# A two-layer encoder on one core: norms ahead of the first product's operands, x loaded by halves, three weight parts on VectorE, and one sum in a tile of its own

## The chip, the core and the metric

One core of one Trainium2 chip runs the whole program. Time is device time of one execution in microseconds (us), taken as the median of several runs. PE is the matmul engine (PEld its weight loads), DVE the vector engine, ACT the scalar engine, POOL GpSimd, SP the engine that issues the DMAs. Each engine works through its own list of instructions in order; an instruction that waits holds up all behind it on that engine.

## What is computed

Two layers on 512 tokens of 1024 channels in float32. Each layer is a half-step feed-forward block, a mixer of four attention kinds, and a second feed-forward block, each followed by a norm:

```python
def _swiglu(h, w_gu, w_down):
    gate, up = jnp.split(h @ w_gu, 2, axis=-1)
    return (jax.nn.silu(gate) * up) @ w_down

for l in range(DEPTH):
    x = _layer_norm(alpha * x + 0.5 * _swiglu(x, ffn_w_gu[l, 0], ffn_w_down[l, 0]), ln_g[l, 0], ln_b[l, 0])
    mix = _token_mixers(x, w_in[l], ..., w_out[l], l)
    x = _layer_norm(alpha * x + mix, ln_g[l, 1], ln_b[l, 1])
    x = _layer_norm(alpha * x + 0.5 * _swiglu(x, ffn_w_gu[l, 1], ffn_w_down[l, 1]), ln_g[l, 2], ln_b[l, 2])
```

`w_gu` is 1024 x 5632, `w_down` 2816 x 1024, `w_in` some 2500 columns wide, `w_out` 1024 x 1024.

## The kernel before

**Numbers.** A float32 product is made of three products of rounded parts: every operand is split into a high part (a cast on ACT: `al`, `wh`, `xTh`) and a low part (operand minus high part, on DVE: `al`, `wl`, `xTl`), and PE adds high·high, high·low and low·high.

**Stages.** Six stages follow one another: ffn(0,0) to about 358 us, mixer 0 to 612, ffn(0,1) to 958, ffn(1,0) to 1320, mixer 1 to 1575, ffn(1,1) to the end. x lies in four tiles of 128 tokens (x_86 to x_89 in the program's names, for t = 0 to 3).

**Gate and up product.** It is done by a seven-product scheme on 2 x 2 blocks. A `Pair(j)` stands for 256 columns of gate and 256 of up; its weights come in four tiles b11, b21 (gate) and b12, b22 (up), 512 KB each. `step1` and `step2` multiply b11 and b21 (banks ga, gb); `step5` first adds b12 to b11 in place (L458), `step6` adds b22 to b11 in place (L467), `step7` adds b22 to b12 (L475), `step3` takes b22, `step4` adds b11 to b21 (L490). Each step splits its operand (`parts4`: ACT cast L403, DVE low part L404, 128x1024 each) and issues 24 matmuls per half, 128x256 wide, spaced 0.12 us apart at full clock. The operands from x, `al[1]` to `al[7]`, are made by `to_al`: tiles t = 0, 1 give `al[1]`, `al[2]` (L181, L182), which steps 1 and 2 use; tiles t = 2, 3 give sums (L216 to L225) and `al[3]` to `al[7]` (L178, L179, L181, L182), which steps 5, 6, 7, 3 and 4 use. p0 and p1 are the pairs 0 and 1. At the start of an ffn the order is p0 steps 1, 2, p1 steps 1, 2, then the rest of p0 and the rest of p1.

**The ring.** `raw_tile` hands out weight buffers in turn; of every seven calls the 1st, 3rd and 5th come from pool `raw` (3 buffers), the others from tag `pt` of pool `blk` (4 buffers). p0 and p1 take eight tiles in the order b11, b21, b12, b22 of p0, then b11, b21, b12, b22 of p1, so seven are free of each other and the eighth reuses the first.

**Into an ffn.** `norm_to_al` (L339) is called for each tile when the stage before has finished it: sum and statistics on DVE (L348, L349, L331, L333), the power on GpSimd (L334, `rs`), one more factor on DVE (L351), the norm itself as two ACT instructions of 128x512 (L353), four PE transposes into `xtp`, and `to_al`. This is so at the entries of ffn(0,1) (called T1 here, about 605 to 660), ffn(1,0) (T2, 950 to 1012) and ffn(1,1) (T3, 1568 to 1625).

**Into a mixer.** The norm has four DVE products per tile (L320 twice, L327 twice), then `to_xT` (transposes, ACT L147, DVE L148). Meanwhile the mixer's first weight units are split; the low parts of units 5, 6 and 7 (`ON_POOL`) run on GpSimd (L239, 128x864, 128x576, 128x1024), the others on DVE.

**Order.** The order on each engine is set by a scheduler that takes the code's order, priorities (`tc.high_priority`) and data into account. At the opening SP loads x_86 and x_87 whole, then p0's four tiles, x_88, x_89, p1's b11 and b21.

## Time and profile before

| | |
|---|---|
| median of 3 runs | 1945.51 us (1944.58 to 1945.53) |
| the profiled execution | 1943.79 us, of which span 1942.0 us |
| PE busy | 1876.5 us, 97% of the span |
| DVE busy | 1697.9 us, 87% |
| ACT busy | 1061.1 us, 55% |
| POOL busy | 262.1 us, 13% |

The span is the profiler's; the 1.8 us between it and the execution's time lie around it. An engine's busy time says how full its list is; whether it is late is seen from the idle time before its instructions, which stands in square brackets in the timeline, with what ended it. PEclk is the share of full TensorE clock that was granted in a stretch: 1.00 is 2.4 GHz, 0.50 is 1.2 GHz.

### The profile page before, as it was taken

How to read it: one execution, taken by the hardware profiler on the slowest of the kernel's cores; microseconds unless marked ns; L12 is line 12 of the kernel's file. 1: busy time of each engine (PE TensorE's matmuls, PEld its weight loads, DVE VectorE, ACT ScalarE, POOL GpSimd, SP SyncE). 2: the span in 40 equal slices, each digit the busy share in tenths (PEclk: the TensorE clock that was granted, in tenths of full speed). 3: DMA queues.
4: the chain of work that ended last, by engine and by line, in shares of the span. 5: the costliest groups of instructions: out<-in, count | busy, mean ns of one | idle time of the engine just before them, and what ended most of it. 6: DMA issues, size and time to landing. Idle time of an engine off the chain costs nothing.

```text
span 1942.0 us, 32394 instructions
## 1 busy us (share of the span) xinstructions
PE 1876.5 (97%) x12252; PEld 1704.2 (88%) x12252; DVE 1697.9 (87%) x2733; ACT 1061.1 (55%) x1851; POOL 262.1 (13%) x387
## 2 busy tenths in 40 slices
PE   7999999999999899999989999999999999999998
PEld 6999998788878899999789999987887879999996
DVE  7999995858998999999499999957689989999985
ACT  5555554247776645555364555532587865455551
POOL 0000000345741000000000000004367300000001
PEclk9999999999999999999999999999999999999999
DMA  6333324243343334233232323241433334144221
GB/s 236 95 123 99 103 66 126 80 115 91 104 104 120 126 93 131 93 93 131 98 115 90 110 94 115 68 143 45 135 90 86 101 125 153 60 130 131 71 83 65
DMA packets 164413, 205.65 MB, mean 106 GB/s; under 512 B 15328, under 2 KB 123872, under 8 KB 164256
## 3 DMA queue, kind: packets, MB, share of 16 engines
q1 hardware_dynamic: 164256, 203.57, 34.0%
q8 instruction: 97, 1.59, 0.3%
q14 instruction: 60, 0.49, 0.1%
HBM read 178.49 MB, written 2.10 MB: 93 GB/s over the span
## 4 chain that ended last, share of the span: by engine, by line
PE 83%; DVE 9%; ACT 3%; POOL 2%; DMA 1%; issue 1%; SPq 0%; DVEq 0%; ACTq 0%; POOLq 0%
PE ga L266 26%; PE gc L266 13%; PE acc L266 9%; PE da L266 7%; PE gb L266 6%; PE nat L266 6%; PE dc L266 3%; PE sc L266 2%; PE pjt L266 2%; PE pv L266 2%; PE ptb L110 2%; PE db L266 2%; PE op L266 2%; DVE p L751 1%; PE xtp L110 1%
## 5 line engine op out<-in xcount | busy, mean ns | idle before, releaser
L403 ACT CAST wh<-b 128x1024 fp32r<-128x1024 f32 x300 | 313.1, 1053 | 287.3 <-DVE b L467 66.5
L266 PE MATMUL ga<-al,wh 128*128 128x256 f32 x2752 | 390.6, 285 | 4.4 <-ACT wh L403 4.4
L266 PEld LDWEIGHTS ga<-al,wh 128*128 128x128 f32 x2752 | 358.4, 192 | 16.1 <-ACT u L471 6.7
L404 DVE TENSOR_TENSOR wl<-b,wh 128x1024 fp32r<-128x1024 f32 x300 | 362.1, 1218 | 4.7 <-ACT wh L403 4.2
L266 PE MATMUL gc<-al,wh 128*128 128x256 f32 x1408 | 206.2, 289 | 20.5 <-ACT al L178 17.5
L266 PE MATMUL ga<-al,wl 128*128 128x256 f32 x1376 | 222.0, 284 | 1.0 <-DVE wl L404 1.0
L334 POOL TENSOR_TENSOR rs<-rs,mhalf 128x1 f32<-128x1 f32 x24 | 19.7, 819 | 1463.9 <-DVE rs L333 1459.7
L266 PEld LDWEIGHTS gc<-al,wh 128*128 128x128 f32 x1408 | 189.3, 197 | 24.3 <-ACT al L178 18.3
L266 PEld LDWEIGHTS ga<-al,wl 128*128 128x128 f32 x1376 | 190.3, 192 | 1.5 <-DVE wl L404 1.5
L540 ACT CAST wh<-d 128x512 fp32r<-128x512 f32 x168 | 98.0, 619 | 85.4 <-PE ga L266 40.8
L266 PE MATMUL acc<-wl,hh 128*128 128x512 f32 x320 | 125.3, 392 | 0.2 <-DVE wl L239 0.2
L266 PE MATMUL acc<-wh,hh 128*128 128x512 f32 x320 | 125.0, 391 | 0.0
L266 PE MATMUL acc<-wh,hl 128*128 128x512 f32 x320 | 124.9, 390 | 0.0
L239 DVE TENSOR_TENSOR wl<-wr,wh 128x1024 fp32r<-128x1024 f32 (+1 forms) x44 | 53.4, 1214 | 77.5 <-ACT wh L238 77.3
L266 PE MATMUL gc<-al,wl 128*128 128x256 f32 x704 | 118.7, 288 | 0.0
L238 ACT CAST wh<-wr 128x1024 fp32r<-128x1024 f32 (+2 forms) x50 | 50.8, 1025 | 109.4 <-PE acc L266 75.6
L541 DVE TENSOR_TENSOR wl<-d,wh 128x512 fp32r<-128x512 f32 x168 | 109.8, 683 | 0.3 <-ACT wh L540 0.2
L266 PE MATMUL da<-wh,dh 128*128 128x512 f32 x384 | 103.9, 392 | 0.0
L266 PEld LDWEIGHTS gc<-al,wl 128*128 128x128 f32 x704 | 101.3, 198 | 0.0
L793 ACT CAST pth<-ptb 128x512 fp32r<-128x512 f32 (+2 forms) x128 | 69.8, 545 | 41.7 <-PE ptb L110 40.5
L266 PE MATMUL gb<-al,wh 128*128 128x256 f32 x640 | 90.8, 283 | 0.5 <-ACT wh L403 0.5
L796 DVE TENSOR_TENSOR ptl<-ptb,pth 128x512 fp32r<-128x512 f32 (+2 forms) x128 | 80.6, 630 | 7.1 <-ACT pth L793 6.6
(320 smaller groups left out, 4148.9 us busy)
## 6 DMA issues: line engine op xcount, KB each, us to landing
b<-in_ffn_w_gu_dram SPq DMA_DIRECT2D x176, 512.0 KB, 4.6
d<-in_ffn_w_down_dram SPq DMA_DIRECT2D x96, 256.0 KB, 3.7
wr<-in_ffn_w_down_dram SPq DMA_DIRECT2D x40, 512.0 KB, 3.2
wr<-in_w_in_dram SPq DMA_DIRECT2D x30, 512.0 KB, 3.7
k<-ph SPq DMA_DIRECT2D x64, 128.0 KB, 2.3
wr<-in_w_out_dram SPq DMA_DIRECT2D x16, 512.0 KB, 3.3
qs<-ph SPq DMA_DIRECT2D x32, 128.0 KB, 2.4
ln_g<-in_ln_g_dram SPq DMA_DIRECT2D x14, 256.0 KB, 3.7
```

The source lines that it names most:

```text
L110: te.transpose(o, a, ident)
L238: se.copy(h[:, w], r[:, w])
L239: (lo or ve).tensor_tensor(l[:, q], r[:, q], h[:, q].bitcast(F32), op=ALU.subtract)
L266: te.matmul(o, a, b, start=start, stop=stop, **kw)
L334: ge.tensor_tensor(rs[:, 1:2], rs[:, 0:1], mhalf[:, 0:1], op=ALU.pow)
L403: se.copy(h, r[:, q])
L404: ve.tensor_tensor(lo, r[:, q], h.bitcast(F32), op=ALU.subtract)
L540: se.copy(wh[:, sl], self.r[rn][q])
L541: ve.tensor_tensor(wl[:, sl], self.r[rn][q], wh[:, sl].bitcast(F32), op=ALU.subtract)
L751: ve.tensor_tensor_reduce(p, sb, nd, -h.slope, h.sink[0] if h.sink else 3.0e38, ALU.add, ALU.min, m)
L793: se.copy(b.ph, b.tb[:, b.k0:b.k1])
L796: ve.tensor_tensor(b.pl, b.tb[:, b.k0:b.k1], b.ph.bitcast(F32), op=ALU.subtract)
```

## The change

1. In `norm_to_al` the sum, statistics and the two ACT instructions of the norm are scheduled with a priority raised by `NORMS = 120`.
2. At the opening, x of tiles 0 and 1 is loaded by halves of the channels (256 KB each): first halves, p0's b11, second halves, p0's b21; then p1's b11 and b21, x_88 and x_89, and p0's b12 and b22. `to_al` takes the groups it is to do, and `enter_half(g)` does one of them for both tiles ahead of step 1 and step 2.
3. `ON_POOL` is empty: the low parts of the mixers' units 5, 6 and 7 are made on DVE.
4. For pairs 0 and 1, `step6` writes its sum into a tile `t2` of its own, taken from the ring, instead of into b11; `step4` reads it there.

```diff
+    NORMS = 120
-    def turned_x(t):
-        bs = []
-        for g in range(2):
+    def turned_x(t, gs=range(2)):
+        for g in gs:
             b = bank4("pt", "xtp")
...
-    def to_al(t, gt=None):
+    def to_al(t, gt=None, gs=range(2)):
...
-            for g, b in turned_x(t):
+            for g, b in turned_x(t, gs):
...
-        stt = sm.tile([P, 2, 6], F32, tag="bn", name="bn", bufs=2)
...
+        with tc.high_priority(NORMS):
+            stt = sm.tile([P, 2, 6], F32, tag="bn", name="bn", bufs=2)
+            xs = [x[t][:, n * FD:(n + 1) * FD] for n in range(2)]
+            for n in range(2):
+                ve.scalar_tensor_tensor(xs[n], accs[n], c * INV_A, xs[n], op0=ALU.mult, op1=ALU.add)
+                ve.bn_stats(stt[:, n], xs[n])
+            rs, mv = norm_factors(stt)
+            ve.tensor_scalar(rs[:, 0:1], mv[:, 0:1], rs[:, 1:2], -1.0, op0=ALU.mult, op1=ALU.mult)
+            for n in range(2):
+                se.activation(xs[n], xs[n], AF.Identity, bias=rs[:, 0:1], scale=rs[:, 1:2])
         to_al(t, gained[0])
...
             def step6(self):
                 r = self.r
-                ve.tensor_tensor(r[11], r[11], r[22], op=ALU.add)
-                w = parts4(r[11])
+                r[6] = raw_tile("t2") if self.j < 2 else r[11]
+                ve.tensor_tensor(r[6], r[11], r[22], op=ALU.add)
+                w = parts4(r[6])
...
-                ve.tensor_tensor(r[21], r[21], r[11], op=ALU.add)
+                ve.tensor_tensor(r[21], r[21], r[6], op=ALU.add)
...
         if opening:
+            half, rest, consts = opening
+            opening.clear()
+            for g, n in ((0, 11), (1, 21)):
+                for t in range(2):
+                    load_half(t, g)
+                p0.load((n,))
+            p1.load((11, 21))
+            for t in range(2, NT):
+                load(x[t], d["x"][0, t * P:(t + 1) * P])
+            p0.load((12, 22))
+            half(0)
+            p0.step1(early[0])
+            half(1)
+            p0.step2(early[1])
+            rest()
+            p1.step1()
+            p1.step2()
+            consts()
...
-        ON_POOL = (5, 6, 7)
+        ON_POOL = ()
...
+    def load_half(t, g):
+        sl = slice(g * FD, (g + 1) * FD)
+        load(x[t][:, sl], d["x"][0, t * P:(t + 1) * P, sl])
+
+    def enter_half(g):
+        for t in range(2):
+            to_al(t, None, (g,))
```

In the changed file most lines of these functions are one further down (L353 becomes L354, L404 becomes L405, L467 becomes L468), while L454 and L458 keep their numbers.

**Mixer 0's entry, DVE**, around the norm of the last tile (x_89). Before:

```order
L316 BN_STATS bn<-x_89 128x6 [waits DVE_49]
L239 TENSOR_TENSOR wl<-wr,wh 128x864 [waits DMAHW7_49,DMAHW0_49]
L331 BN_AGGR mv<-bn 128x2 [waits DVE_49]
L333 TENSOR_SCALAR rs<-mv 128x1 [waits DVE_49]
L320 SCALAR_TENSOR_TENSOR x_89<-x_89,mv,ln_g 128x512 x2
L327 SCALAR_TENSOR_TENSOR x_89<-x_89,rs,ln_b 128x512 [waits DVE_49,Pool_49]
L327 SCALAR_TENSOR_TENSOR x_89<-x_89,rs,ln_b 128x512 [waits DVE_49]
```

Now:

```order
L316 BN_STATS bn<-x_89 128x6 [waits DVE_49]
L239 TENSOR_TENSOR wl<-wr,wh 128x864 [waits DMAHW2_49,DMAHW1_49]
L331 BN_AGGR mv<-bn 128x2 [waits DVE_49]
L239 TENSOR_TENSOR wl<-wr,wh 128x864 [waits DMAHW4_49,DMAHW3_49]
L333 TENSOR_SCALAR rs<-mv 128x1 [waits DVE_49]
L320 SCALAR_TENSOR_TENSOR x_89<-x_89,mv,ln_g 128x512 x2
L327 SCALAR_TENSOR_TENSOR x_89<-x_89,rs,ln_b 128x512 [waits DVE_49,Pool_49]
L327 SCALAR_TENSOR_TENSOR x_89<-x_89,rs,ln_b 128x512 [waits DVE_49]
L239 TENSOR_TENSOR wl<-wr,wh 128x576 [waits DMAHW6_49,DMAHW5_49]
L239 TENSOR_TENSOR wl<-wr,wh 128x1024 [waits DMAHW7_49,Activation_49]
```

Three low parts have come to DVE, one ahead of the four products of x_89's norm and two behind them; on GpSimd the three L239 rows are gone and the powers L334 follow one another. Mixer 1's entry reads the same.

**T2, DVE**, the norm factors of x_89 (L331, L333, then L351 before and L352 now) and the operands around them. Before:

```order
L331 BN_AGGR mv<-bn 128x2 [waits DVE_49]
L404 TENSOR_TENSOR wl<-b_10992,wh 128x1024 [waits Activation_49]
L179 TENSOR_TENSOR al_10594<-t_10814,al_10594 128x4x128 [waits Activation_49]
L220 TENSOR_TENSOR ac<-ac,t_10814 128x512 [waits DVE_49]
L333 TENSOR_SCALAR rs<-mv 128x1 [waits DVE_49]
L454 TENSOR_TENSOR s_10954<-gb,s_10954 128x512 [waits PE_49,Activation_49]
L225 TENSOR_TENSOR ac<-ac 128x512 [waits DVE_49]
L179 TENSOR_TENSOR al_10595<-ac,al_10595 128x4x128 [waits Activation_49]
L179 TENSOR_TENSOR al_10596<-t_10809,al_10596 128x4x128 [waits Activation_49]
L182 SCALAR_TENSOR_TENSOR al_10593<-a_10804,al_10593 128x4x128 [waits Activation_49]
L179 TENSOR_TENSOR al_10606<-ac,al_10605 128x2x128 [waits Activation_49]
L351 TENSOR_SCALAR rs<-mv,rs 128x1 [waits Pool_49]
```

Now:

```order
L349 SCALAR_TENSOR_TENSOR x_89<-acc_10370,x_89 128x512 [waits PE_49]
L350 BN_STATS bn<-x_89 128x6 [waits DVE_49]
L331 BN_AGGR mv<-bn 128x2 [waits DVE_49]
L333 TENSOR_SCALAR rs<-mv 128x1 [waits DVE_49]
L216 TENSOR_TENSOR t_10820<-t_10815,a_10810 128x512 [waits Activation_49]
L352 TENSOR_SCALAR rs<-mv,rs 128x1 [waits Pool_49]
L218 TENSOR_TENSOR t_10815<-t_10815,ac 128x512 [waits DVE_49]
L405 TENSOR_TENSOR wl<-b_10998,wh 128x1024 [waits Activation_49]
```

Between the aggregate and the last factor stood ten instructions, now two; the sum for p1's step 5 (L458) and the group of `al` parts stand behind.

**T1, DVE**, around the norm factors of x_88 (L333, L351; now L333, L352). Before:

```order
L333 TENSOR_SCALAR rs<-mv 128x1 [waits DVE_49]
L349 BN_STATS bn<-x_89 128x6 [waits DVE_49]
L182 SCALAR_TENSOR_TENSOR al_6952<-ac,al_6951 128x2x128 [waits DMAHW0_49,Activation_49]
L351 TENSOR_SCALAR rs<-mv,rs 128x1 [waits Pool_49]
L475 TENSOR_TENSOR b_7223<-b_7223,b_7225 128x1024 [waits DMAHW4_49]
L182 SCALAR_TENSOR_TENSOR al_6954<-ac,al_6953 128x2x128 [waits DMAHW6_49,DMAHW7_49,DMAHW0_49,Activation_49]
L348 SCALAR_TENSOR_TENSOR x_89<-op,x_89 128x512 [waits PE_49]
```

Now:

```order
L333 TENSOR_SCALAR rs<-mv 128x1 [waits DVE_49]
L468 TENSOR_TENSOR t_7397<-b_7223,b_7229 128x1024 [waits DMAHW6_49]
L352 TENSOR_SCALAR rs<-mv,rs 128x1 [waits Pool_49]
L350 BN_STATS bn<-x_89 128x6
L182 SCALAR_TENSOR_TENSOR al_6954<-ac,al_6953 128x2x128 [waits DMAHW1_49,DMAHW0_49,Activation_49]
L476 TENSOR_TENSOR b_7227<-b_7227,b_7229 128x1024
L349 SCALAR_TENSOR_TENSOR x_89<-op,x_89 128x512 [waits PE_49]
L182 SCALAR_TENSOR_TENSOR al_6956<-ac,al_6955 128x2x128 [waits DMAHW2_49,Activation_49]
L350 BN_STATS bn<-x_89 128x6 [waits DVE_49]
L182 SCALAR_TENSOR_TENSOR al_6958<-ac,al_6957 128x2x128 [waits DMAHW1_49,DMAHW2_49,DMAHW0_49,Activation_49]
L331 BN_AGGR mv<-bn 128x2 [waits DVE_49]
L491 TENSOR_TENSOR b_7225<-b_7225,t_7397 128x1024
```

The sums for p0's steps 6 and 4 (L468, L491) stand beside that of step 7 (L476) among the low parts of `al[1]` and `al[2]` of tile 1; before, L467 and L490 came 26 and 28 rows behind L475.

**T1, SP**: the weight loads of p1 (b_7298 and b_7296 are its b21 and b11, b_7519 its b12; now b_7302, b_7300 and b_7524, and b_7526 is its b22). Before, the three stood together:

```order
L94 DMA b_7298<-in_ffn_w_gu_dram 128x4x256 [waits DMAHW6_49,DVE_49,PE_49]
L94 DMA b_7296<-in_ffn_w_gu_dram 128x4x256 [waits DMAHW7_49,DMAHW1_49,DVE_49]
L94 DMA b_7519<-in_ffn_w_gu_dram 128x4x256 [waits DMAHW0_49,PE_49]
L94 DMA ln_b<-in_ln_b_dram 128x512
L94 DMA d<-in_ffn_w_down_dram 128x512 [waits DMAHW2_49]
```

Now, at that place and 13 rows further on:

```order
L96 DMA b_7302<-in_ffn_w_gu_dram 128x4x256 [waits DMAHW0_49,DVE_49,PE_49]
L96 DMA b_7300<-in_ffn_w_gu_dram 128x4x256 [waits DMAHW3_49,DMAHW1_49,DVE_49]
L96 DMA ln_b<-in_ln_b_dram 128x512 [waits DMAHW2_49]
L96 DMA d<-in_ffn_w_down_dram 128x512
L96 DMA d<-in_ffn_w_down_dram 128x512 [waits DMAHW4_49]
```

```order
L96 DMA ln_g<-in_ln_g_dram 128x512 [waits DMAHW5_49,DVE_49]
L96 DMA d<-in_ffn_w_down_dram 128x512 [waits DMAHW6_49,DVE_49,Activation_49]
L96 DMA b_7524<-in_ffn_w_gu_dram 128x4x256 [waits DMAHW7_49,DVE_49]
L96 DMA d<-in_ffn_w_down_dram 128x512 [waits DMAHW0_49,DVE_49]
L96 DMA b_7526<-in_ffn_w_gu_dram 128x4x256 [waits DMAHW1_49,DVE_49,PE_49]
```

The tile `t2` takes the ring's seventh buffer, which was that of p1's b12; b12 and b22 of p1 now reuse buffers of p0's b11 and b21 and are loaded after these are done with.

## Rows read from the trace of the kernel before

**Rows 1.** Page: busy time, share of the span and instructions of each engine.

```profile
PE 1876.5 (97%) x12252; PEld 1704.2 (88%) x12252; DVE 1697.9 (87%) x2733; ACT 1061.1 (55%) x1851; POOL 262.1 (13%) x387
```

**Rows 2.** Windows: stretch, length, busy time and count per engine, clock, DMA, GB/s.

```profile
0.00:20.00 20.00, 12.81 (x79) 11.88 (x80) 9.12 (x17) 11.56 (x22) 0.19 (x4) 1.00 0.94 340
...
366.00:369.00 3.00, 2.75 (x9) 2.40 (x10) 2.90 (x6) 0.59 (x1) 0.00 (x0) 0.50 0.29 84
...
643.00:649.00 6.00, 5.49 (x26) 5.35 (x26) 6.00 (x10) 4.56 (x8) 0.00 (x0) 0.50 0.60 182
...
700.00:800.00 100.00, 99.30 (x717) 93.67 (x716) 99.09 (x128) 50.73 (x71) 0.00 (x0) 1.00 0.32 100
```

**Rows 3.** DVE timeline at mixer 0's entry: start, duration, instruction, [idle before].

```profile
355.74 1.41 DVE L327 SCALAR_TENSOR_TENSOR x<-x,rs,ln_b 128x512 f32<-128x512 f32 x2
...
361.77 4.33 DVE L327 SCALAR_TENSOR_TENSOR x<-x,rs,ln_b 128x512 f32<-128x512 f32 x2
...
369.20 1.04 DVE L239 TENSOR_TENSOR wl<-wr,wh 128x864 fp32r<-128x864 f32 x1
...
371.78 1.41 DVE L327 SCALAR_TENSOR_TENSOR x<-x,rs,ln_b 128x512 f32<-128x512 f32 x2
375.24 0.69 DVE L148 TENSOR_TENSOR xTl<-xtp,xTh 128x512 fp32r<-128x512 f32 x1 [2.05 <-ACT xTh L147]
```

**Rows 4.** POOL timeline at mixer 0's entry.

```profile
361.64 3.91 POOL L239 TENSOR_TENSOR wl<-wr,wh 128x864 fp32r<-128x864 f32 x2
```

**Rows 5.** PE timeline at mixer 0's entry, its three groups of transposes that matter.

```profile
364.43 0.63 PE L110 MATMUL xtp<-ident,x 128*128 128x128 f32 x4 [1.45 <-DVE x L327]
366.25 1.09 PE L110 MATMUL xtp<-ident,x 128*128 128x128 f32 x4 [1.19 <-DVE x L327]
...
373.98 0.60 PE L110 MATMUL xtp<-ident,x 128*128 128x128 f32 x4
```

**Rows 6.** PE timeline of the opening, three instructions with idle time before them.

```profile
4.84 3.73 PE L110 MATMUL xtp<-ident,x 128*128 128x128 f32 x16 [4.84 <-DMA x<-in_x_dram]
10.92 2.78 PE L266 MATMUL ga<-al,we 128*128 128x256 f32 x10 [2.35 <-ACT we L403]
...
30.14 1.10 PE L266 MATMUL gc<-al,wh 128*128 128x256 f32 x7 [0.82 <-DVE al L179]
```

**Rows 7.** Page: DMA issues of the ffn's weights, KB each, median us to landing.

```profile
b<-in_ffn_w_gu_dram SPq DMA_DIRECT2D x176, 512.0 KB, 4.6
d<-in_ffn_w_down_dram SPq DMA_DIRECT2D x96, 256.0 KB, 3.7
```

**Rows 8.** DVE timeline of the opening: the low parts after p0's step 5 sum.

```profile
37.36 4.62 DVE L404 TENSOR_TENSOR wl<-b,wh 128x1024 fp32r<-128x1024 f32 x4
```

**Rows 9.** DVE timeline at T2.

```profile
949.61 1.23 DVE L458 TENSOR_TENSOR b<-b,b 128x1024 f32<-128x1024 f32 x1 [1.87 <-DMA b<-in_ffn_w_gu_dram]
...
976.96 0.69 DVE L348 SCALAR_TENSOR_TENSOR x<-acc,x 128x512 f32<-128x512 f32 x1
...
982.91 0.15 DVE L333 TENSOR_SCALAR rs<-mv 128x1 f32<-128x1 f32 x1
...
986.31 0.20 DVE L351 TENSOR_SCALAR rs<-mv,rs 128x1 f32<-128x1 f32 x1
```

**Rows 10.** PE timelines of T1 and T2, four instructions with idle time before them.

```profile
622.28 2.65 PE L266 MATMUL ga<-al,we 128*128 128x256 f32 x20 [0.45 <-DVE al L182]
...
642.55 0.58 PE L266 MATMUL gc<-al,wh 128*128 128x256 f32 x1 [5.25 <-ACT al L178]
...
993.81 0.58 PE L266 MATMUL gc<-al,wh 128*128 128x256 f32 x1 [4.43 <-ACT al L178]
995.51 1.86 PE L266 MATMUL gc<-al,wh 128*128 128x256 f32 x7 [1.11 <-DVE al L179]
```

**Rows 11.** DVE timeline at T1: one sum of 128x1024.

```profile
619.02 1.22 DVE L475 TENSOR_TENSOR b<-b,b 128x1024 f32<-128x1024 f32 x1
```

**Rows 12.** Line L334, the power on GpSimd: count, shortest/median/longest in ns, first and last start.

```profile
L334 POOL TENSOR_TENSOR rs<-rs,mhalf x24: 550/897/1473, 347.4 to 1936.4; 128x1 f32<-128x1 f32 x24
```

More of the change, by code (lines that the diff above doesn't have):

```diff
@@ L140, in turned_x @@
                 tr(b[:, k], x[t][:, (4 * g + k) * P:(4 * g + k + 1) * P])
-            bs.append(b)
             yield g, b
@@ L344, in norm_to_al @@
             gained[:] = [gt]
-        stt = sm.tile([P, 2, 6], F32, tag="bn", name="bn", bufs=2)
-        xs = [x[t][:, n * FD:(n + 1) * FD] for n in range(2)]
-        for n in range(2):
-            ve.scalar_tensor_tensor(xs[n], accs[n], c * INV_A, xs[n], op0=ALU.mult, op1=ALU.add)
-            ve.bn_stats(stt[:, n], xs[n])
-        rs, mv = norm_factors(stt)
-        ve.tensor_scalar(rs[:, 0:1], mv[:, 0:1], rs[:, 1:2], -1.0, op0=ALU.mult, op1=ALU.mult)
-        for n in range(2):
-            se.activation(xs[n], xs[n], AF.Identity, bias=rs[:, 0:1], scale=rs[:, 1:2])
+        with tc.high_priority(NORMS):
[8 more added lines that the diff above has]
+                se.activation(xs[n], xs[n], AF.Identity, bias=rs[:, 0:1], scale=rs[:, 1:2])
         to_al(t, gained[0])
@@ L427, in __init__, with load @@
                 self.j, self.w, self.r = j, {}, {}
-            def load(self, gate=True, up=True):
+            def load(self, ns=(11, 21, 12, 22)):
                 j = self.j
-                for n, k, u in ((11, 0, 0), (21, 1, 0), (12, 0, 1), (22, 1, 1)):
-                    if not (up if u else gate):
-                        continue
+                for n in ns:
+                    k, u = n // 10 - 1, n % 10 - 1
                     self.r[n] = raw_tile(f"b{n}")
@@ L589, in ffn @@
         if opening:
-            opening.pop(0)()
-        p0.load()
-        p0.step1(early[0])
-        p0.step2(early[1])
-        if opening:
-            opening.pop(0)()
-        p1.load(up=False)
-        p1.step1()
-        p1.step2()
-        if opening:
-            opening.pop(0)()
+            half, rest, consts = opening
[16 more added lines that the diff above has]
+            consts()
+        else:
+            p0.load()
+            p0.step1(early[0])
+            p0.step2(early[1])
+            p1.load((11, 21))
+            p1.step1()
+            p1.step2()
         for step in p0.rest():
             step()
-        p1.load(gate=False)
+        p1.load((12, 22))
         for step in p1.rest():
@@ L1624, in mixer, with enter_rest @@
         flush()
-    def enter(ts):
-        for t in ts:
-            load(x[t], d["x"][0, t * P:(t + 1) * P])
-        for t in ts:
+    def load_half(t, g):
[4 more added lines that the diff above has]
+            to_al(t, None, (g,))
+    def enter_rest():
+        for t in range(2, NT):
             to_al(t)
@@ L1636, in tile_encoder @@
     new_al()
-    opening = [lambda: enter((0, 1)), lambda: enter((2, 3)), constants]
+    opening = [enter_half, enter_rest, constants]
     for l in range(DEPTH):
```

## The prediction

> **What bounds the kernel now.** I read first the busy times, then the windows, then the idle times on each engine at the places that the change touches. PE is busy 1876.5 of 1942.0 us [rows 1], so at most 65.5 us of waiting can be won, and all of it at the seams of the stages: inside a feed-forward stage PE has 99.30 of 100 us at clock 1.00, with DVE beside it at 99.09 of 100 [rows 2]. So DVE is as full as PE there; what DVE loses in those stages is not made up. The places that matter are the opening, the two entries of the mixers, and T1, T2 and T3. The second thing to see is the clock: after idle time of 1.45 and 1.19 us [rows 5] the stretch 366 to 369 was granted 0.50, that is 1.2 instead of 2.4 GHz, and after 5.25 us [rows 10] the stretch 643 to 649 was too [rows 2]. So idle time is paid for twice. All sums are made against the profiled execution, 1943.79 us; the median of the runs shown is 1.7 us above it.
>
> **Three low parts to VectorE.** At mixer 0's entry the last two products of x_88's norm take 4.33 us; the same pair takes 1.41 before and after it [rows 3]. The difference, 2.92 us, lies under two L239 on GpSimd, 361.64 to 365.55 [rows 4]. PE waits for just these products, 1.45 + 1.19 = 2.64 us [rows 5]. Then it works at half clock: of the 2.75 us that it is busy in 366 to 369 [rows 2] about half, 1.4, is lost. That is 4.0 us; mixer 1 repeats these rows, so it is 8.0 for both, 8.1 with the last few tenths of the low clock. The edit takes GpSimd's products away, so the products of the norm should take 1.41 again. What comes onto DVE is one part of 128x864, 1.04 us [rows 3], one of 128x576 (0.7 by its size) and one of 128x1024 (1.22, as any of that size [rows 11]). Only the first stands ahead of x_89's norm. That norm ended at 373.19 [rows 3]; it now ends 2.92 sooner and about 0.95 later, at 371.2. PE transposed x_89 from 373.98, without waiting [rows 5]; 4.0 us less and four matmuls more ahead of it in the new order (0.2 each) bring it there at about 370.8 for the first half and 371.3 for the second, when they are ready. So the next wait is 0 to 0.1; if PE is there first, up to 0.9 per mixer. The other two parts fall into the 2.05 us in which DVE sat idle [rows 3]; without that cover they would cost 1.9 each time. **Mixers: -8.1, bounds -5 to -8.5.**
>
> **T2: norms ahead.** x_89's second sum starts at 976.96, but its statistics end only at 982.91, and the factor that ACT waits for comes at 986.31 [rows 9], because ten instructions stand between. Now two do: aggregate, L333, one 0.68 us sum, factor. That gives the factor at 976.96 plus 0.69 for the sum, as much for its statistics, 0.2 for the small ones and 0.9 for the power [rows 12], near 979.4, and the norm and the transposes of x_89 some 6.7 us sooner. The products of steps 1 and 2 end where they did (993.81 less 4.43, 989.4), since they hang on earlier tiles; PE then waited 4.43 + 1.11 us for the first sum of tiles 2 and 3 [rows 10]. Those operands are cast and subtracted in a list of some ten DVE and ACT instructions each, so they come not 6.7 but 3.3 us sooner (992.2 against 995.5). With the clock as low as before that is the gain, less 0.4 for a low part behind the later load (below): 2.9; with the clock kept, the other 23 matmuls of step 5 would save 0.1 us each, the spacing of 0.13 at full clock (2.65 us for 20 [rows 10]) against about twice that: another 2.3. **T2: -2.9, bounds -5 to 0.**
>
> The power on GpSimd took 550 to 1473 ns [rows 12], so its length depends on what runs beside it, and the new order puts a DVE sum right behind L333. The Trainium skill ("SBUF — State Buffer", section "SBUF: two separate sides") says that GpSimd and a DVE instruction with two SBUF inputs exclude each other for the whole instruction. By that rule the power starts only after the 0.68 us sum, x_89's factor is 0.3 later, and T2 would be -2.6; the trace agrees with it in the mixer's rows (3, 4), but my sum uses the median length.
>
> **T1 and T3: norms and sums in the wrong place.** Here the norm of x_87 and the sums for p0 go ahead of operands of the first product. Three sums of 1.22 us [rows 11] stand among the low parts of tile 1, where one stood: +2.3 us on DVE, and x_87's norm on ACT stands ahead of casts that it used to follow. I work the first product out to start at 626 instead of 622.3 [rows 10]: 3.7 later. Steps 1 and 2 then end at 641.5 (before at 642.55 less 5.25, 637.3). But x_88 and x_89 are normed sooner, so step 5's operands are there at 641.6, and the wait of 5.25 us [rows 10] is gone; p0's step 4 ends 2.4 us sooner at full clock. Against this: the idle time is now at 621 to 626, about as long as the 5.25 that brought 0.50 [rows 2], so I charge 1.9 of the 2.3 us for slow matmuls; and 1.0 for p1's loads (below). Net +0.5, and the same for T3, whose rows repeat T1's. **T1 and T3: +0.5 each, bounds -3 to +4 each.**
>
> **The opening.** PE starts at 4.84 on x and begins the first product at 10.92 after a wait for ACT [rows 6]. A 512 KB weight lands in 4.6 us, a 256 KB one in 3.7 [rows 7], so the half of x is there about 1 us sooner. Ahead of step 1 ACT now has half of the copies and splits, so the product can start near 8.1. p0's and p1's steps 1 and 2 end 3.1 us sooner, step 5 only 0.8 sooner than 30.14 [rows 6], as its operands hang on DVE's and ACT's lists. With the sum in its own tile p0's step 4 ends 3.7 us sooner. Then p1's b22 must wait for p0's b21 buffer, which is free after the last of the four low parts, 41.98 [rows 8], 1 us less now; plus 4.6 to land, plus sum, cast and low part, 1.2 + 1 + 1.2 with the queue ahead: PE waits 2.0. Net -1.9. **Opening: -1.9, bounds -5 to +2.**
>
> The Trainium skill ("DMA: Bandwidth & Descriptors", section "Bandwidth") fits a transfer at some 2 us plus its bytes over 436 GB/s. By that, an estimate, a half is only 0.6 us quicker than a whole, and the opening would be -1.5 instead of -1.9. The rows' 0.9 includes queues, so the rule may be nearer.
>
> **The later loads of p1.** The tile t2 takes the buffer in which p1's b12 lay early. p1's b12 and b22 are now issued when p0's buffers come free, and DVE's sums for p1 (L458, L468) wait for a landing of 4.6 us [rows 7] with DVE's whole list behind them: low parts, the operands of steps 5 to 4, sums of gb. The trace has one such wait, 1.87 us [rows 9]. In the four gate products I allow PE 2.0 (opening), 1.0 (T1), 0.4 (T2) and 1.0 (T3), counted above. From below: 0, where the load lands under work; from above the whole 4.6 at each.
>
> **Sum.** -8.1 - 2.9 + 0.5 + 0.5 - 1.9 = -11.9: 1943.8 becomes 1931.9, and the median 1945.5 becomes about 1933.5.
>
> **The rivals.** (a) *The clock holds.* At T1, T2 and T3 the idle time falls into pieces, after which full clock is kept: another 2.3 at T2 and 1.9 at T1 and T3, 6.1 in all: 1927.5. For it: at the opening 2.35 us of idle time before 10.92 [rows 6] left the clock at 1.00 [rows 2]. Against it: 1.45 and 1.19 was enough at the mixer. (b) *The transitions give back.* p1's loads and the reordered lists cost T1, T3 and the opening 2 us each more than I allow, and T2 gives nothing: 1933.5 + 6 + 2.9 = 1942.4 at the worst, 1939 as its middle; the mixers alone stay. For it: DVE's list has no slack there. (c) *Slower: DVE stands behind loads.* If DVE waits for p1's loads about the whole landing in all four gate products with PE behind it, the cost is 4 x 4.6 = 18.4 instead of 4.4, so -11.9 turns into +2 and the time into 1947.5; with the loads queued behind others, at 6 us each, it is 24, and the time 1953. It decides from 5 us per place, as 11.9 + 3.9 + 4.4 = 20.2. Against it: of all such sums the trace has one that waited for its load, and 1.87 us at that [rows 9]. (d) *The mixer's stall stays.* GpSimd's products were not the cause, or x_89 becomes the wait: only half of the 8.1 comes, 1937.5. Against it: the same products at 1.41 twice beside an idle GpSimd.
>
> **How the numbers follow.** Forecast (1930 to 1937) 0.50; (a) 0.15; (b) 0.20; (d) 0.07; (c) 0.08. The predicted time is the forecast's, 1933.5. The range for 8 in 10 takes in (a)'s centre and most of (b): 1926.5 to 1941.5. A measurement of this kernel tells about 0.2%, 3.9 us, from no change: faster means below 1941.6. That holds for the forecast, (a), (d) and four fifths of (b), 0.86 with a little off for what I did not see; same is the rest of (b) and a third of (c), 0.08; slower 0.06.
>
> **What would show it.** Right: L327 at 1.41 three times in each mixer's entry, no PE idle time at x_88's transposes, clock 1.00 there; x_89's factor at T2 three instructions behind its second sum; the wait ahead of gc at T1 gone, and one of 4 to 5 us ahead of the first ga in its place; PE idle time at p1's steps 5 and 6 released by low parts, DVE idle time released by DMA ahead of L458 or L468. Wrong: idle time of PE at x_89's transposes in the mixers; waits of DVE on b loads above 3 us in each gate product; or T1 and T3 each longer or shorter by over 4 us.

## The result

The changed kernel takes 1924.99 us (1924.08 to 1928.49, four runs) against 1945.52 (1944.58 to 1947.37): ratio 0.9897, 95% interval 0.9879 to 0.9914. That is 20.5 us, where 12 were predicted, and 1.5 us below the low end of the range.

A part of this is not seen when the two profiles are laid side by side: the profiled execution of before, 1943.79, is the fastest of its runs, that of the changed kernel, 1928.49, the slowest of its four. They stand 15.3 us apart. Runs of one kernel differ, and a lower mean granted clock goes with a longer run: the changed kernel had 0.988 (1928.49) to 0.992 (1924.08), before in the comparisons below 0.983 (1952.18) to 0.989 (1944.43). One execution, of run u_t2 below, took 4680 us and is left out of every figure. In the table a second trace of the changed kernel (run a_again below, 1926.39) stands beside the first. The table is made from the starts of the same DVE instructions in two traces (the first product of each pair's output, the norms' aggregates, the low parts in the mixers); a stage's term is what the distance between the traces grew by in it. Where two traces have the same code, such terms differ by up to 1.2 us at T1, T2 and T3 (the two columns here), by more in the mixers, and by 3.0 us in the opening (o_pool below, which leaves the opening as it was, against before).

| place | predicted | first trace | second trace |
|---|---|---|---|
| opening, to the end of ffn(0,0) | -1.9 | -2.9 | -3.3 |
| mixer 0, entry | -4.05 | -4.6 | -3.7 |
| mixer 0, the rest | 0 | +2.3 | +0.9 |
| T1, ffn(0,1) | +0.5 | +0.5 | -0.7 |
| T2, ffn(1,0) | -2.9 | -5.2 | -4.9 |
| mixer 1 | -4.05 | -4.4 | -4.7 |
| T3, ffn(1,1) | +0.5 | -0.9 | -0.9 |
| sum | -11.9 | -15.2 | -17.3 |

### The profile page after: what moved, and what is told of

Same layout as the page of the kernel before. It is cut to its first block, busy times and chain, and to the rows that moved or that the text cites. A ratio compares the mean times of both kernels' runs of the same rounds, so it can differ in the third digit from the quotient of the medians.

```text
span 1926.7 us, 32397 instructions
## 1 busy us (share of the span) xinstructions
PE 1875.4 (97%) x12252; PEld 1704.4 (88%) x12252; DVE 1696.6 (88%) x2739; ACT 1061.6 (55%) x1851; POOL 251.6 (13%) x381
## 4 chain that ended last, share of the span: by engine, by line
PE 63%; DVE 9%; ACT 2%; POOL 1%; DMA 1%; issue 1%; SPq 0%; DVEq 0%; POOLq 0%; ACTq 0%
PE ga L266 19%; PE gc L266 9%; PE acc L266 7%; PE da L266 5%; PE gb L266 4%; PE nat L266 3%; PE sc L266 3%; PE dc L266 3%; PE pjt L266 2%; PE ptb L112 2%; PE pv L266 2%; PE db L266 1%; DVE p L766 1%; DMA b<-in_ffn_w_gu_dram 1%; PE op L266 1%
## 5 line engine op out<-in xcount | busy, mean ns | idle before, releaser
L404 ACT CAST wh<-b 128x1024 fp32r<-128x1024 f32 x292 | 303.8, 1051 | 255.2 <-DVE b L468 61.1
L405 DVE TENSOR_TENSOR wl<-b,wh 128x1024 fp32r<-128x1024 f32 x292 | 351.8, 1217 | 3.3 <-ACT wh L404 3.0
L334 POOL TENSOR_TENSOR rs<-rs,mhalf 128x1 f32<-128x1 f32 x24 | 21.6, 901 | 1457.0 <-DVE rs L333 1449.0
L239 DVE TENSOR_TENSOR wl<-wr,wh 128x1024 fp32r<-128x1024 f32 (+2 forms) x50 | 59.4, 1188 | 78.5 <-ACT wh L238 78.5
```

Source lines behind the costliest of these rows:

```text
L239: (lo or ve).tensor_tensor(l[:, q], r[:, q], h[:, q].bitcast(F32), op=ALU.subtract)
L334: ge.tensor_tensor(rs[:, 1:2], rs[:, 0:1], mhalf[:, 0:1], op=ALU.pow)
L404: se.copy(h, r[:, q])
L405: ve.tensor_tensor(lo, r[:, q], h.bitcast(F32), op=ALU.subtract)
```

## The profile after

The page's first row answers to [rows 1]: PE is as busy as before in a span that is 15.3 us shorter.

```profile
PE 1875.4 (97%) x12252; PEld 1704.4 (88%) x12252; DVE 1696.6 (88%) x2739; ACT 1061.6 (55%) x1851; POOL 251.6 (13%) x381
```

**Mixer 0's entry**, DVE timeline, answers to [rows 3]. The pair L327 of x_88 takes 1.41 us, the three added low parts 1.01, 0.75 and 1.23.

```profile
358.88 1.41 DVE L327 SCALAR_TENSOR_TENSOR x<-x,rs,ln_b 128x512 f32<-128x512 f32 x2
...
364.27 1.01 DVE L239 TENSOR_TENSOR wl<-wr,wh 128x864 fp32r<-128x864 f32 x1
...
366.58 1.41 DVE L327 SCALAR_TENSOR_TENSOR x<-x,rs,ln_b 128x512 f32<-128x512 f32 x2
367.91 0.75 DVE L239 TENSOR_TENSOR wl<-wr,wh 128x576 fp32r<-128x576 f32 x1
368.99 1.23 DVE L239 TENSOR_TENSOR wl<-wr,wh 128x1024 fp32r<-128x1024 f32 x1 [0.33 <-ACT wh L238]
```

PE timeline of the same place, answers to [rows 5]: none of the transposes waits, neither x_88's (eight at 359.94) nor x_89's.

```profile
359.94 1.12 PE L112 MATMUL xtp<-ident,x 128*128 128x128 f32 x8
...
367.76 0.60 PE L112 MATMUL xtp<-ident,x 128*128 128x128 f32 x4
368.43 0.60 PE L112 MATMUL xtp<-ident,x 128*128 128x128 f32 x4
```

**T2**, DVE timeline, answers to [rows 9]. The sums for p0's steps 6, 7 and 4 (L468, L476, L491) are made at 947 to 952, before the norms; the norm of x_89 needs 2.89 us from the start of its second sum (L349) to that of its last factor (L352), where it needed 9.35. But the first sum of x_89 for step 5 (L216) starts 9.8 us behind that factor.

```profile
944.92 1.23 DVE L458 TENSOR_TENSOR b<-b,b 128x1024 f32<-128x1024 f32 x1 [1.84 <-DMA b<-in_ffn_w_gu_dram]
947.19 1.22 DVE L468 TENSOR_TENSOR t<-b,b 128x1024 f32<-128x1024 f32 x1
948.93 1.22 DVE L476 TENSOR_TENSOR b<-b,b 128x1024 f32<-128x1024 f32 x1
951.25 1.22 DVE L491 TENSOR_TENSOR b<-b,t 128x1024 f32<-128x1024 f32 x1
...
971.11 0.69 DVE L349 SCALAR_TENSOR_TENSOR x<-acc,x 128x512 f32<-128x512 f32 x1
...
974.00 0.21 DVE L352 TENSOR_SCALAR rs<-mv,rs 128x1 f32<-128x1 f32 x1 [0.45 <-POOL rs L334]
...
983.76 0.68 DVE L216 TENSOR_TENSOR t<-t,a 128x512 f32<-128x512 f32 x1
```

PE's idle time at T2 ahead of gc (the last two lines) is 1.35 + 0.77 us, against 4.43 + 1.11 [rows 10]; at T1 (the lines above them) the 5.25 ahead of gc is gone, and waits ahead of transposes, for low parts (L405) and for `al` parts have come. In sum PE's waits of over 0.15 us at T1 (600 to 680 us) fell only from 8.3 to 7.2 us, at T2 (930 to 1045) from 7.6 to 3.1.

```profile
617.94 0.90 PE L112 MATMUL xtp<-ident,x 128*128 128x128 f32 x4 [2.63 <-ACT ac L200]
619.91 0.58 PE L266 MATMUL ga<-al,we 128*128 128x256 f32 x1 [0.85 <-DVE al L182]
633.44 0.74 PE L266 MATMUL ga<-al,wl 128*128 128x256 f32 x4 [2.14 <-DVE wl L405]
...
639.94 1.10 PE L266 MATMUL ga<-al,wh 128*128 128x256 f32 x7 [0.76 <-DVE al L179]
641.67 0.89 PE L266 MATMUL gc<-al,wl 128*128 128x256 f32 x4 [0.64 <-DVE wl L405]
...
985.15 0.38 PE L266 MATMUL gc<-al,wh 128*128 128x256 f32 x1 [1.35 <-ACT al L178]
986.30 1.44 PE L266 MATMUL gc<-al,wh 128*128 128x256 f32 x7 [0.77 <-DVE al L179]
```

**The later loads of p1.** The view of waits of DVE (line and releaser: us in total, times, longest) has two lines for sums that waited for a weight.

```profile
DVE b L458 <- DMA b<-in_ffn_w_gu_dram: 2.4, 2, 1.8
DVE t L468 <- DMA b<-in_ffn_w_gu_dram: 1.4, 2, 1.1
```

The 1.8 us among them are those at 944.92 above: p0's first sum, which waited as long before [rows 9]. What p1's sums waited is 0.53 us at T2, 1.09 at T3 (both below, DVE timeline) and 0.31 at T1, 1.9 us in all. PE has no idle time at p1's steps 5 and 6 in any ffn.

```profile
982.62 1.23 DVE L458 TENSOR_TENSOR b<-b,b 128x1024 f32<-128x1024 f32 x1 [0.53 <-DMA b<-in_ffn_w_gu_dram]
...
1603.40 1.23 DVE L468 TENSOR_TENSOR t<-b,b 128x1024 f32<-128x1024 f32 x1 [1.09 <-DMA b<-in_ffn_w_gu_dram]
```

**The opening**, PE timeline, answers to [rows 6]. The first transposes come 0.85 us sooner, the first product (10.61) only 0.3 sooner, since the transposes of the second half stand ahead of it and wait; step 5 begins even 0.65 later.

```profile
3.99 2.23 PE L112 MATMUL xtp<-ident,x 128*128 128x128 f32 x8 [3.99 <-DMA x<-in_x_dram]
9.02 1.94 PE L112 MATMUL xtp<-ident,x 128*128 128x128 f32 x8 [2.79 <-ACT we L404]
10.61 4.63 PE L266 MATMUL ga<-al,we 128*128 128x256 f32 x24
...
30.79 1.86 PE L266 MATMUL gc<-al,wh 128*128 128x256 f32 x7 [0.62 <-DVE al L179]
39.06 1.22 PE L266 MATMUL ga<-al,wh 128*128 128x256 f32 x8 [0.68 <-ACT u L472]
```

## The experiments

Ratios are to the kernel before in the same comparison, with 95% intervals; a part of the gain is the difference of two such ratios. "Changed" is 0.9897 above and 0.9888 (0.9874 to 0.9901) in its second comparison.

### One part taken back at a time

**Low parts on GpSimd again**, from the changed kernel:

```diff
-        ON_POOL = ()
+        ON_POOL = (5, 6, 7)
```

> The changed kernel with the low parts of the mixers' units 5, 6 and 7 back on GpSimd; all else as changed. Theory (GpSimd's products stop the norm's, and PE pays idle time and low clock): the pair L327 of x_88 takes about 4.3 us again in both mixers, PE idles 1.4 and 1.2 us at x_88's transposes, and the time rises by 8 to 10 us to 1933 to 1935. Rival (the stall was a matter of order, and the other parts of the change have moved it away): L327 at 1.4 us and a rise of 0 to 3 us.

1936.44 us, ratio 0.9942 (0.9928 to 0.9956): some 9 to 11 us of the gain go. The picture of before is back; the timelines of DVE, POOL and PE in turn:

```profile
358.36 4.33 DVE L327 SCALAR_TENSOR_TENSOR x<-x,rs,ln_b 128x512 f32<-128x512 f32 x2
```

```profile
358.23 3.92 POOL L239 TENSOR_TENSOR wl<-wr,wh 128x864 fp32r<-128x864 f32 x2
```

```profile
361.03 0.63 PE L112 MATMUL xtp<-ident,x 128*128 128x128 f32 x4 [1.48 <-DVE x L327]
362.84 1.09 PE L112 MATMUL xtp<-ident,x 128*128 128x128 f32 x4 [1.19 <-DVE x L327]
```

**Norms without the raised priority:**

```diff
-        with tc.high_priority(NORMS):
+        if True:
```

> The changed kernel without the raised priority of the norms. Theory (the norms' place makes T2's gain): x_89's factor at T2 comes some 6 us later again, PE waits 4 to 5 us ahead of gc there, and the kernel is 4 to 7 us slower, 1929 to 1932, nearly all of it at T2; T1 and T3 within 2 us. Rival (the sum's own tile makes the gain, since it lets the sums of steps 6 and 4 go early): within 2 us of the changed kernel.

1923.75 us, ratio 0.9879 (0.9865 to 0.9892). The theory falls: without the part that should have made T2's gain the kernel is not slower.

**The sum in place:**

```diff
-                r[6] = raw_tile("t2") if self.j < 2 else r[11]
+                r[6] = r[11]
```

> The changed kernel with step 6's sum in place on b11 again, so that the ring is as before. Theory of the prediction (the later loads of p1 cost 4.4 us, the earlier sum gains about as much in the opening alone): within 3 us of the changed kernel, faster at T1 and T3 by about 1 us each, slower in the opening by 1 to 2. Rival (the later loads cost nothing, since PE has no idle time at p1's steps 5 and 6 in the changed kernel's trace): slower by 2 to 6 us, with no place where it is faster.

1934.66 us, ratio 0.9933 (0.992 to 0.9947): 7 to 9 us of the gain go. The theory falls; the rival holds, and the loss is above the 2 to 6 us that it gave. The trace is of a second run of this kernel:

> The changed kernel with step 6's sum in place, again, for its trace: waits of PE ahead of gc at T2 of 3 us or more and of about 4 to 5 at T1 and T3, as before the change, if the own tile is what removed them; time 1932 to 1935.

1932.98 us, ratio 0.9928 (0.9909 to 0.9946), 6 to 8 us of the gain. PE timeline at T1, T2 and T3:

```profile
640.85 1.23 PE L266 MATMUL gc<-al,wl 128*128 128x256 f32 x4 [4.32 <-DVE wl L405]
...
987.35 0.38 PE L266 MATMUL gc<-al,wh 128*128 128x256 f32 x1 [2.42 <-ACT al L178]
...
1598.35 1.22 PE L266 MATMUL gc<-al,wl 128*128 128x256 f32 x4 [4.32 <-DVE wl L405]
```

At T1 and T3 the wait of 4.3 us is for step 5's low part, and behind it on DVE stand the two sums in place (L468 at 641.85, L491 at 643.59); at T2 it is 2.4, less than expected. Placed against the traces of the changed kernel, T3 loses 3 to 4 us, T2 2 and T1 about 1.

**x whole again**, with the loads in the old order:

```diff
-            for g, n in ((0, 11), (1, 21)):
-                for t in range(2):
-                    load_half(t, g)
-                p0.load((n,))
...
+            whole()
+            p0.load()
             p0.step1(early[0])
-            half(1)
             p0.step2(early[1])
             rest()
+            p1.load((11, 21))
```

> The changed kernel with x of tiles 0 and 1 loaded whole and the opening's order of loads as before. Theory (terms add up): p0's step 4 and all behind it come 2 to 4 us later, time 1927 to 1929. Rival (what the opening wins is given back at p1's late b22): no change beyond 1 us.

1929.41 us, ratio 0.9912 (0.9898 to 0.9925): 3 to 5 us of the gain go, 2.7 to 3.0 of them in the opening by the traces. The theory holds. The edit takes back the halves and the new order of loads together; which of the two gains is not shown. PE at step 5 of p0:

```profile
31.83 0.58 PE L266 MATMUL gc<-al,wh 128*128 128x256 f32 x1 [4.47 <-ACT al L178]
33.00 1.86 PE L266 MATMUL gc<-al,wh 128*128 128x256 f32 x7 [0.59 <-DVE al L179]
```

### One part alone

Three kernels from the one before, each with one of the edits:

```diff
+                r[6] = raw_tile("t2") if self.j < 2 else r[11]
-                ve.tensor_tensor(r[11], r[11], r[22], op=ALU.add)
-                w = parts4(r[11])
+                ve.tensor_tensor(r[6], r[11], r[22], op=ALU.add)
+                w = parts4(r[6])
```

> The kernel before with one edit: step 6's sum of pairs 0 and 1 in a tile of its own. Theory (the sum's own tile makes the gain at the entries of the ffns, whatever the norms' place): 8 to 11 us faster than before, 1935 to 1938, with the waits of 4 to 5 us ahead of gc at T1, T2 and T3 shorter by 3 or more each and no new wait of PE for p1's loads. Rival (it pays only where the norms go first, since DVE has no idle time to take the early sums otherwise): within 3 us of before. The prediction's own term for it was a loss of 4.4 us in late loads against a gain in the opening: about 2 us slower to 1 us faster.

1930.64 us, ratio 0.9917 (0.9904 to 0.9929): 16 us by this edit alone, where the theory had 8 to 11. The rival falls. The trace, of the slowest of its five runs (1935.53), shows 8.3 of them. Its DVE has the sums at 952, 954 and 956 us, ahead of T2's norms, and PE's wait ahead of gc there is 0.64 us. At T1, and the same at T3, a new wait as long as the old one stands ahead of p1's step 2, for a cast: there the theory's shorter waits did not come. This is PE's timeline:

```profile
643.13 2.07 PE L266 MATMUL gb<-al,wh 128*128 128x256 f32 x8 [5.60 <-ACT wh L403]
...
989.96 1.10 PE L266 MATMUL gc<-al,wh 128*128 128x256 f32 x7 [0.64 <-DVE al L179]
```

```diff
-        ON_POOL = (5, 6, 7)
+        ON_POOL = ()
```

> The kernel before with one edit: the low parts of the mixers' units 5, 6 and 7 on VectorE. Theory (about 4.0 to 4.6 us at each mixer's entry): 8 to 10 us faster than before. Rival (half of it comes back as a wait for x_89 or in the mixer): 3 to 5 us.

1937.97 us, ratio 0.9952 (0.9938 to 0.9965): 9.3 us. The theory holds.

```diff
+        with tc.high_priority(120):
             stt = sm.tile([P, 2, 6], F32, tag="bn", name="bn", bufs=2)
...
```

> The kernel before with one edit: the raised priority of the norms. The prediction's theory (x_89's factor at T2 comes 6 us sooner and takes 3 us off the wait ahead of gc): 2 to 4 us faster, all of it at T2. Theory now, after the run without the priority was not slower: within 2 us of before, since the operands behind the norm hang on ACT's and DVE's lists and not on the norm.

1946.63 us, ratio 0.9998 (0.9989 to 1.0006). Nothing. But not nothing at each place: in the trace, to the end of each ffn, T2 gains 3.2 us (PE waits 2.42 + 0.41 us ahead of gc), while T1 and T3 lose 2.1 and 1.7. At T1, and the same at T3, a new wait stands:

```profile
649.95 1.23 PE L266 MATMUL gc<-al,wl 128*128 128x256 f32 x4 [4.32 <-DVE wl L405]
...
996.73 0.38 PE L266 MATMUL gc<-al,wh 128*128 128x256 f32 x1 [2.42 <-ACT al L178]
997.52 1.86 PE L266 MATMUL gc<-al,wh 128*128 128x256 f32 x7 [0.41 <-DVE al L179]
```

So the prediction's mechanism at T2 is there when the norms go first alone; it is the sum over the three places that is near zero (+0.7 us).

And the changed kernel beside them, unedited:

> The changed kernel again, beside the single edits and for a second trace. If the low clock at 536 to 543 us of its first trace is chance, this trace lacks it or has it elsewhere and the mixers' stages together are 2 to 3 us shorter; if it belongs to the kernel, it is there again. Time 1924 to 1928.

1925.37 us, ratio 0.9888 (0.9874 to 0.9901). Windows of 536 to 543 us in the first and the second trace of the changed kernel:

```profile
536.00:543.00 7.00, 6.09 (x23) 5.60 (x23) 6.88 (x24) 5.21 (x17) 1.94 (x2) 0.52 0.46 131
```

```profile
536.00:543.00 7.00, 5.69 (x28) 5.32 (x29) 6.88 (x22) 5.32 (x17) 1.72 (x2) 0.76 0.39 119
```

The clock was 0.52 in one and 0.76 in the other, on the same list of instructions; in the trace of before this place had no low clock in mixer 0, but it did in mixer 1 (0.76 from 1503 to 1510 us). It falls in some executions and for different lengths, on short idle times of PE (ahead of pv, for low parts, up to 2.2 us) that both kernels have.

### What in the own tile gains

Three kernels from before. First the ring's shift alone (the sum stays in place):

```diff
             def step6(self):
+                if self.j < 2:
+                    ve.memset(raw_tile("t2")[:, 0:1], 0.0)
```

> The kernel before, with a tile drawn from the ring in step 6 of pairs 0 and 1 and only its first column set to zero, so that p1's b12 and b22 move to the buffers of p0's b11 and b21 as in the changed kernel, while the sum stays in place on b11. Theory (the gain of the own tile comes from the sums of steps 6 and 4 going early, freed from the low part of b11): no gain, 0 to 4 us slower than before for the later loads. Rival (the gain comes from the ring's shift, which moves p1's loads and its sum L458 out of the way of the operands): most of the 16 us of the single edit is there.

1945.15 us, ratio 0.9987 (0.9978 to 0.9996): 2 us faster, where the theory had 0 to 4 slower. The rival falls, though at T2 the shift has a part: the wait ahead of gc is 1.02 + 1.02 there and the stage gains 2.6 us, since p1's sum (977.57 before, 1005.02 here) and p0's last one (989.37 before, 1001.25 here) no longer stand in the way. T3 loses 0.9.

Then the own tile without the shift, as two half tiles with another tag:

```diff
+                if self.j < 2:
+                    r[6] = [block("hl", "t2") for _ in range(2)]
+                    for q in range(2):
+                        ve.tensor_tensor(r[6][q], r[11][:, q * 512:(q + 1) * 512], r[22][:, q * 512:(q + 1) * 512], op=ALU.add)
```

> The kernel before, with step 6's sum of pairs 0 and 1 in two half tiles of another pool (tag hl), so that it is not in place and the ring is not shifted; each sum is two instructions of 128x512. Theory: most of the gain of the single edit, 8 to 16 us faster than before. Rival (ring's shift): within 3 us of before.

1933.01 us, ratio 0.9927 (0.9914 to 0.9939): 14 us. So most of it is the tile and not the shift. PE's wait ahead of gc at T1 is shorter by only 0.9 us:

```profile
639.86 0.38 PE L266 MATMUL gc<-al,wh 128*128 128x256 f32 x1 [4.36 <-ACT al L178]
```

Last the own tile from the ring, with its sum held behind step 5's low part, as it was in place:

```diff
                 r[6] = raw_tile("t2") if self.j < 2 else r[11]
+                if self.j < 2:
+                    ve.tensor_scalar(r[6][:, 0:1], self.lo5[:, 0, 0:1].bitcast(F32), 1.0, None, op0=ALU.mult)
```

> The kernel before with step 6's sum of pairs 0 and 1 in a tile of its own from the ring, but first one column of that tile is written from step 5's low part (128x1, 0.1 us), so that the sum stands behind that low part as it did in place. Theory (the gain is that the sums of steps 6 and 4 run early, in DVE's idle time under the norms, and so do not stand among the operands of tiles 2 and 3): the gain of the own tile is gone, within 4 us of before. Rival (the gain is that the tile is not overwritten, so that casts and low parts of b11 wait for nothing): 10 to 16 us faster than before, as with the own tile alone.

1946.12 us, ratio 0.9995 (0.9985 to 1.0004). The gain is gone. DVE of this kernel at T1: the sum stands at 642.69 among the operands of x_89, as it did in place (the first two lines, from the trace of before: L467 and L490, with x_89's first sum L216 behind them at 641.11).

```profile
638.50 1.22 DVE L467 TENSOR_TENSOR b<-b,b 128x1024 f32<-128x1024 f32 x1
...
639.97 1.22 DVE L490 TENSOR_TENSOR b<-b,b 128x1024 f32<-128x1024 f32 x1
```

```profile
642.69 1.23 DVE L471 TENSOR_TENSOR t<-b,b 128x1024 f32<-128x1024 f32 x1
```

The waits ahead of gc do not tell this kernel from the half tiles: at T1 it waits 4.30 us there, they 4.36. Its loss comes later, where PE waits again, at 768 (the second line below), 1117 and 1729 us, 1.9 us each time, against 0.7, 0 and 0.7 before.

```profile
645.61 0.38 PE L266 MATMUL gc<-al,wh 128*128 128x256 f32 x1 [4.30 <-ACT al L178]
...
767.93 1.21 PE L266 MATMUL ga<-al,wh 128*128 128x256 f32 x8 [1.62 <-ACT wh L403]
```

What does tell them apart is DVE's idle time. In the table it is summed over three stretches, from the first norm's aggregate at T1, T2 and T3 to the first output of the seventh pair (together 596 us before, with DVE idle for 30.6); both columns are differences to before, in us, from the traces.

| kernel | length | DVE idle |
|---|---|---|
| o_pool (no edit in these stages) | +0.6 | +0.4 |
| norms alone (o_norms) | +1.5 | +2.6 |
| ring's shift alone (ring_only) | -0.6 | +1.0 |
| own tile, sum held (own_late) | -0.5 | +1.3 |
| changed, two traces | -6.9, -7.9 | -2.6, -3.4 |
| half tiles (own_hl) | -8.6 | -7.0 |
| own tile alone (o_t2) | -12.2 | -9.1 |
| changed without the priority, two traces | -14.9, -13.4 | -11.4, -9.7 |

So what gains is that the sums of steps 6 and 4 can run early, in time that DVE else sits idle. In place, the sum must follow the low part of b11, and the order then has it and L490 in the middle of the operands of the last tile; in a tile of its own it needs only its inputs, which lie in SBUF long before, and is made while DVE waits for norms. That fits DVE's 99.09 of 100 us inside an ffn [rows 2]: there it has no slack to make a sum that it did not make at the entry. The lengths follow the idle time, but not one for one: the kernels with early sums gain 1.6 to 4.5 us more than their idle time fell by, and why is not shown.

### Which of GpSimd's products

From the changed kernel:

```diff
-        ON_POOL = ()
+        ON_POOL = (7,)
```

> The changed kernel with the low part of unit 7 alone (128x1024) on GpSimd. Theory (what stops the norm is GpSimd's product beside it in time, here only those of units 5 and 6): as the changed kernel within 1.5 us, with L327 at 1.41 us and unit 7's product at about 2.4 us on GpSimd, beside DVE's idle time. Rival (any of the three on GpSimd costs): 3 to 4 us slower.

1926.61 us, ratio 0.9894 (0.9876 to 0.9912), as the changed kernel. GpSimd's one product takes 2.40 us and the pairs L327 of x_88 and x_89 take 1.41 each. It is the two products beside the norm in time that cost, not GpSimd's work as such.

```profile
369.51 2.40 POOL L239 TENSOR_TENSOR wl<-wr,wh 128x1024 fp32r<-128x1024 f32 x1 [2.72 <-ACT wh L238]
```

### A version that beats both

The changed kernel without the raised priority, again:

> The changed kernel without the raised priority of the norms, again, to tell whether it beats the changed kernel: 1921 to 1925 against 1925 for the changed one. Theory: 1 to 4 us faster than the changed kernel, since the early norm puts x_87's two ACT instructions and their transposes ahead of operands of the first product at T1 and T3. Rival: the same within 1 us.

1922.84 us, ratio 0.9874 (0.9861 to 0.9887). Its eight runs in two comparisons lie at 1920.6 to 1924.7, those of the changed kernel at 1924.1 to 1928.5; the intervals of the ratios overlap, so 2 us between these two is likely and not certain. Against before it is the fastest kernel of this study. At T2 its one wait ahead of gc is 0.64 us, at T1 and T3 it has 5.6 us at p1's step 2 instead of the changed kernel's spread of waits. PE at T1 and T2:

```profile
635.12 2.08 PE L266 MATMUL gb<-al,wh 128*128 128x256 f32 x8 [5.61 <-ACT wh L404]
...
981.80 1.10 PE L266 MATMUL gc<-al,wh 128*128 128x256 f32 x7 [0.64 <-DVE al L179]
```

## Why the prediction was wrong

**Right: the mixers.** 8.1 predicted, 9.3 by the single edit, 4.4 to 4.7 at mixer 1 in the traces. GpSimd's two products were the cause (u_pool, pool7), x_89 did not become the next wait, and the two parts behind its norm were covered. Rivals (b) and (d) are out: the transitions gave back no more than the +0.5 that was forecast, and the stall is gone.

**Wrong: the own tile.** This is the step that failed. The tile had no line of its own in the sum. Its cost stood in it as 4.4 us of late loads in four places, and its early sums as a cost at T1 and T3 ("among the low parts of tile 1, where one stood: +2.3 us on DVE"); a credit for them stood in the opening alone (p0's step 4 3.7 us sooner, step 5 0.8). By the runs the tile is worth 16 us alone and 6 to 9 as the last part; in its own trace (o_t2) T1, T2 and T3 gain 2.4, 6.1 and 2.3 us.

Two parts of the step were wrong. First, the late loads: p1's sums waited 1.9 us for them in all, PE nothing, because p1's steps 5 and 6 stand behind all of p0's rest; the 2.0 us at p1 in the opening and the 1.0 at T1 and T3 were not there, and at T2 the shift gained 2.6 us (ring_only) where 0.4 were charged. The wait of 1.87 us [rows 9] that the prediction took as its example was ahead of p0's sum; p1's, at 977.57, waited for nothing. Rival (c) rested on the same step. Second, the early sums: at T1, T2 and T3 I charged them where they now stand and credited nothing for DVE's idle time that they fill. The two sums of 1.22 us each stood among the operands of x_89 and are gone from there; before, DVE had idled 4.83 us at T1 ahead of the first sum of x_88.

**Wrong in its cause: T2.** -2.9 was forecast for the norms and -5 came. The norms alone do give 3.2 there (o_norms), as worked out. In the changed kernel they add nothing: without them T2 gains 6.1 us (u_norms, u_norms2) instead of 5. x_89's factor was early by 6.5 us, nearly the 6.7 predicted, and L216 started 9.8 us behind it: the operands hang on DVE's and ACT's lists. What failed here is the first reading: the wait ahead of gc was read as the norm's, where after the early sums it is the list's. Beside the 0.68 us sum x_89's power on GpSimd took 0.84 us, against 0.55 for the tile before it with DVE idle: 0.3 longer, which the prediction had worked out and left out of its sum.

**T1 and T3** were put at +0.5 each; +0.5 and -0.7, and -0.9 twice came. The first product was late as worked out: in the frame of before it went on at 626.2 (621.0 plus the 5.2 us won earlier), where 626 was given; the wait ahead of it came as 2.63 + 0.85 us instead of 4 to 5. But that the wait ahead of gc goes was credited to the norms, and the norms alone leave 4.32 us there (o_norms), the own tile alone 5.60 ahead of gb (o_t2). Under the small sum lie larger terms of both signs: 2 to 4 us won by the early sums (o_t2, u_norms), about 2 lost by the norms' place (o_norms). That they cancel is luck.

**The opening** came out at -2.9 and -3.3 for -1.9. The trace of before is a weak measure of it: PE's first wait there ended at 4.84 us, the earliest of the eight traces with x loaded whole (up to 6.07), and o_pool, with the same opening, is 3.0 us behind it at the end of this stage. So o_t2, 1.3 behind, does not show that the own tile costs anything here. By the run with x whole (u_open) the halves and their order of loads are worth 3 to 5 us. The single steps were worse than the sum: the first product started at 10.61 and not near 8.1, since the transposes of x's second half stand ahead of it and wait (for ACT in this trace, for x itself in those of u_norms, u_t2b and pool7); step 5 came later, not sooner. What is gained is seen beside u_open: there step 5 goes on at 33.00 and not at 30.79, as the operands of the last tile come 1.9 us later (its L216 at 30.11 against 28.19, behind a wait for ACT). Which instruction on ACT makes the difference is open. The first half of x started PE at 3.99 to 4.50 us in seven traces, a whole one at 4.84 to 6.07: some 1.0 us between the middles, nearer the rows' 0.9 than the 0.6 of the Trainium skill's fit, though the groups scatter by 0.5 and 1.2. That fit stands in "DMA: Bandwidth & Descriptors", section "Anatomy of one DMA — SWDGE (gpsimd) path", and is for transfers that GpSimd issues; here SP issues them.

**The range** ended at 1926.5. Rival (a), 1927.5, names the clock at T2: after 1.35 + 0.77 us of idle time the stretch 986 to 990 was granted 0.61 and 990 to 992 0.94, so the clock still fell, for about half as long as before (0.50 from 994 to 1000).

```profile
986.00:990.00 4.00, 3.70 (x19) 3.70 (x20) 4.00 (x7) 3.27 (x7) 0.00 (x0) 0.61 0.53 161
990.00:992.00 2.00, 2.00 (x18) 2.00 (x18) 2.00 (x4) 1.15 (x2) 0.00 (x0) 0.94 0.76 223
```

What (a) says happened in part, and by shorter idle time, not by the clock holding; at T1 it did not, with 0.51 from 618 to 625. The traces account for 3 to 5 us of the miss of 8.5. The rest is the base: I put the sum against a profiled execution at the fast end of before's runs, and the medians stand 5 us farther apart than the first two traces. An early landing of x in that execution may be a part of this; where the rest lies is not shown.

## What to carry to other kernels

An operation in place on a buffer that others still read is an order, not only a saving of memory: ask which instruction it must follow, where that puts it in its engine's list, and whether it could run in that engine's idle time if it had a tile of its own. When a change moves work forward, credit the place that it leaves as fully as you charge the place that it goes to. And where several parts act on one wait, cost each alone and as the last one, because here one part's 3 us at T2 were worth nothing or less once another had removed the same wait.
